# A hybrid encoder trunk: the first half of q's products moved between two pairs of modulation blocks

## The chip, the cores and the metric

The kernel runs on one core of one Trainium2 chip. The metric is the device time of one execution in microseconds (us); lower is better. A core has a matrix engine (TensorE, PE in the profile; its weight loads are PEld), a vector engine (VectorE, DVE), a scalar engine (ScalarE, ACT), a third elementwise engine (GpSimd, POOL) and an engine that issues transfers (SyncE, SP). Each works through its own instructions in the order in which they stand, and waits where an instruction needs a result of another engine or a transfer.

## What is computed

Two layers over 256 tokens of width 1024. In each layer a vector `c` gives six modulation vectors, the normalised input is scaled and shifted with two of them, and projected by one wide matrix; q and k of the recurrent branch are the first columns of that projection.

```python
cond = jax.nn.silu(c)
for l in range(DEPTH):
    mod = cond @ w_ada[l] + b_ada[l]
    shift1, scale1, gate1, shift2, scale2, gate2 = ...
    h = rms_norm(x, norm1_g[l]) * (1 + scale1) + shift1
    proj = h @ w_in[l] + b_in[l]
    ...
    x = x + gate1 * (merged @ w_out[l])
    h2 = rms_norm(x, norm2_g[l]) * (1 + scale2) + shift2
    x = x + gate2 * hierarchical_moe(h2, ...)
return rms_norm(x, final_norm_g)
```

Between the projection and `merged` stand a short convolution and a gated recurrence on q, k and v, a grouped attention, and a merge of both; the mixture of experts has 32 experts of width 512.

## The kernel before

A weight matrix is kept in tiles of 1 MB (128 partitions x 2048 numbers). `plan` is one list of all weight loads in the order of their use; `pump` issues them on SP's queue as buffers come free. A load also waits for the load that stands eight places ahead of it (the four that ACT issues at the start are among the eight).

**The opening of layer 0.** `shift1` and `scale1` are each two blocks of 512 columns; `FIRST = (0, 2, 1, 3)` is the order of the four blocks: the first half of shift, the first half of scale, then the two second halves. For each block `ada_fast` runs `ada_sums` (L415): two weight tiles, four products of 32 x 512 with each, into the tile `pada`; ACT copies it to the buffer `t` (L431). `columns` (L438) turns such a row into four columns of a tile `pcol` with two-column products on PE, and `ada_put` (L449) adds the bias and writes them to `c1b` on DVE. PE also transposes the input (`turn_rows`, L487, four tiles `pxt`) and spreads the norm's factor over the partitions (`spread`, L687).

**build(ks)** makes the modulated input for the row blocks k of 128 channels, as a high part `hh` and a low part `hl` (what the high part's rounding leaves): DVE scales the transposed rows (L700), ACT adds the shift and rounds (L701). For even k, DVE makes the low part (L706); for odd k, ACT makes the full sum (L703) and POOL subtracts the high part from it (in `low`, L501). Blocks 0 to 3 need the modulation blocks 0 and 2, blocks 4 to 7 need 1 and 3. In the order below `hh` and `hl` are the buffers R_141 and R_142 of the kernel before.

**dense(1)** does one step of the projection. `prep` takes half a weight tile through one of two spare buffers (R_143 and R_144): ACT rounds it to its high part (L520), DVE and POOL each subtract one half to get the low part (L501). Then PE makes 24 products (`chan`, L560): high weight x `hh`, high weight x `hl`, low weight x `hh`, each for two column groups o and four blocks k. Two steps (`kh` 0 and 1) cover blocks 0 to 3 and 4 to 7 of one pair of column groups. The first four steps of layer 0 are ordered q's first pair with blocks 0 to 3, q's second pair with blocks 0 to 3, and then both with blocks 4 to 7. Of the two weight tiles the first serves the first two steps. In this text the four are steps 1 to 4. When a pair is complete, `fin_qk` runs: ACT adds a bias (L592), ACT and DVE do a convolution of five taps (L594, L596), and ACT the silu (L598).

What sets the order: PE and SP follow the order in which the code is written (`MANUAL`); ACT, DVE and POOL are ordered by a scheduler, which `tc.high_priority` tells what to put first. `MIX` lists, for each layer, how many dense steps stand between the other pieces of work; its first entry for layer 0 is 3, of which one step was already done in the opening. PSUM tiles come in two groups of four buffers: tag "f" for products and modulation sums, tag "c" for the rest (`pxt` among them).

Of the kernel before, what the change touches and what calls it, by code (L numbers as in the profile page):

```python
# [18 lines left out]
P = 128  # L19
# [47 lines left out]
def trunk(ctx, tc, x, c, b_ada, b_in, mlstm_norm_g, norm2_g, final_g,  # L67
# [211 lines left out]
    for l in range(depth):  # L279
        if l == 0:  # L280
            for b in FIRST:
                plan_ada(0, b)
        else:
            plan_ada(l, EARLY[0])
        for it in stream(l):
            if it[0] in DENSE:
                sh = (8, 256) if it[0] == "akv" else (4, 512)
                add((it[0], l, *it[1:]), in_t[l, W_IN.index(it)].rearrange("p (k c) -> p k c", k=sh[0]), sh)
            elif it[0] == "r":
                plan_ada(l, it[1])  # L290
            else:
                plan_ada(l + 1, it[1])
# [116 lines left out]

    def ada_sums(l, b):  # L410
        pb = ps.tile([P, 512], F32, tag="f", name="pada")
        for h in range(2):
# [14 lines left out]

    def ada_fast(b):

        t = rot("fast", 5, 0, 2, 512)  # L430
        A.copy(t, ada_sums(0, b))  # L431
        return t

    def columns(t):

        pc = ps.tile([P, 512], F32, tag="f", name="pcol")
        for j in range(4):
            T.matmul(pc[:, 2 * j:2 * j + 2], lhsT=t[:, P * j:P * j + P], rhs=ones[:, 0:2], start=True, stop=True)  # L438
        return pc[:, 0:8].rearrange("p (j o) -> p j o", o=2)[:, :, 0]
# [7 lines left out]

    def ada_put(c1, cols, b, t):
        V.tensor_tensor(c1[:, 4 * b:4 * b + 4], columns(t), cols[:, 80 + 4 * b:84 + 4 * b], op=ALU.add)  # L449

# [39 lines left out]
    def mixer(l, p):  # L490
# [185 lines left out]
        if l == 0:  # L676
            fast = {FIRST[0]: ada_fast(FIRST[0])}
        else:
# [30 lines left out]
        if l == 0:  # L709
            cols = p["cols"]  # L710
            spread()
            fast[FIRST[1]] = ada_fast(FIRST[1])
            for b in FIRST[:2]:
                ada_put(c1, cols, b, fast[b])
            build(range(4))
            for b in FIRST[2:]:
                fast[b] = ada_fast(b)
            with tc.high_priority():
                for b in FIRST[2:]:
                    ada_put(c1, cols, b, fast[b])  # L720
                build(range(4, 8))
            dense(1)
            withhold([("a", s) for s in ONCE])
# [320 lines left out]
        for i, w in enumerate(MIX[l].split()):  # L1044
            if w.isdigit():
                for _ in range(int(w) - (i == 0)):
                    step()
# [548 lines left out]
```

## Time and profile before

| | |
|---|---|
| median of 3 runs | 1459.84 us (1457.97 to 1459.91) |
| the profiled execution's own time | 1458.14 us |
| its span, first to last instruction | 1456.4 us |
| mean granted TensorE clock | 0.974 |
| PE busy | 1324.0 us (91%) |
| DMA | 521.29 MB, mean 358 GB/s |

A profile is one execution. Its rows name the engine, the line, the operation, output and inputs by the program's names, and how many instructions stand in the row. In a timeline a row begins with its start and its length, and ends with the idle time of its engine just before and what released it. In views by stretch the columns are the busy time of each engine with its count of records, the granted clock (1.00 is 2.4 GHz, 0.50 is 1.2 GHz), the busy share of the DMA engines and what they moved. A product in 32-bit mode shows as two records; the rounded ones of L560 show as one.

### The profile page before, as it was taken

To read this page: it belongs to the slowest core of one execution; us is meant where nothing else is said; L and a number is where in the kernel's file an instruction comes from. 1 tells how busy PE (TensorE), PEld (TensorE's weight loads), DVE (VectorE), ACT (ScalarE), POOL (GpSimd) and SP (SyncE) were. 2 spreads that over 40 slices of the span, in tenths; PEclk is the share of its full clock that TensorE was granted. 3 is DMA by queue.
4 is the path that set the end of the run, shared out by engine and by line. 5 is a ranking of instruction groups with operands and counts; after the bars stand their busy time and mean duration, and the time that the engine had idled before them with its cause. 6 is when DMAs were issued, how large, how long until landed. Compare 5 with 4: busy or idle time off the path is not lost. (4 is left out here: it accounts for less than half of the span.)

```text
span 1456.4 us, 19790 instructions
## 1 busy us (share of the span) xinstructions
PE 1324.0 (91%) x7836; PEld 771.7 (53%) x7837; DVE 615.3 (42%) x1376; ACT 403.4 (28%) x755; POOL 264.5 (18%) x297
## 2 busy tenths in 40 slices
PE   6899999799999989789889999997999998987996
PEld 3788779734443434234359788893443443433432
DVE  3686756613323223212268776653323232223223
ACT  3636564411111101101046366542111111101111
POOL 2553336200000000000045533550000000000000
PEclk9999999899999999999999999998999999999998
DMA  9866594899999999999996556459999999999995
GB/s 385 350 267 251 234 366 170 329 387 424 426 427 424 425 428 425 425 384 416 424 415 239 227 188 241 178 232 370 426 425 424 428 425 425 427 425 424 373 427 231
DMA packets 50148, 521.29 MB, mean 358 GB/s; under 512 B 6656, under 2 KB 6656, under 8 KB 9344
## 3 DMA queue, kind: packets, MB, share of 16 engines
q1 hardware_dynamic: 48576, 515.94, 85.9%
q0 software_dynamic: 608, 2.14, 0.4%
q10 hardware_dynamic: 864, 1.85, 0.3%
q8 instruction: 65, 1.06, 0.3%
q14 instruction: 35, 0.29, 0.1%
HBM read 518.86 MB, written 1.05 MB: 357 GB/s over the span
## 5 line engine op out<-in xcount | busy, mean ns | idle before, releaser
L1300 PE MATMUL pgu<-arena 128*64 128x512 f32 x1376 | 325.9, 599 | 19.7 <-DMA arena<-in_gate_t_dram 12.6
L1300 PEld LDWEIGHTS pgu<-arena 128*64 128x64 f32 x1376 | 104.4, 138 | 232.1 <-issue 196.5
L1324 PE MATMUL pd<-arena 128*64 128x512 f32 x800 | 195.5, 595 | 21.8 <-ACT arena L1315 21.8
L1309 DVE SCALAR_TENSOR_TENSOR arena<-pgu,wsl,arena 128x512 f32<-128x512 f32 x32 | 24.0, 751 | 381.1 <-PE pgu L1300 381.1
L1256 POOL TENSOR_TENSOR arena<-oh,arena 128x256 f32<-128x256 f32 x32 | 19.5, 615 | 728.4 <-DVE oh L1250 465.5
L579 PE MATMUL pd<-R,R 128*128 128x256 f32 x1056 | 138.6, 290 | 3.3 <-DVE arena L619 1.7
L579 PEld LDWEIGHTS pd<-R,R 128*128 128x128 f32 x1056 | 132.3, 196 | 10.9 <-issue 6.1
L560 PE MATMUL pd<-R,R 128*128 128x256 f32 x1008 | 132.0, 289 | 4.7 <-ACT R L520 3.6
L501 POOL TENSOR_TENSOR R<-arena,R 128x512 fp32r<-128x512 f32 (+1 forms) x74 | 113.6, 1536 | 121.9 <-ACT R L520 88.7
L1324 PEld LDWEIGHTS pd<-arena 128*64 128x64 f32 x800 | 60.0, 137 | 137.5 <-issue 107.9
L560 PEld LDWEIGHTS pd<-R,R 128*128 128x128 f32 x1008 | 125.2, 194 | 13.9 <-issue 5.3
L1335 DVE TENSOR_TENSOR y<-pd,arena 128x512 f32<-128x512 f32 x64 | 44.1, 692 | 198.0 <-PE pd L1324 167.1
L1336 ACT CAST yh<-y 128x512 fp32r<-128x512 f32 x64 | 39.6, 619 | 235.5 <-DVE y L1335 235.5
L1300 PE MATMUL pgu<-B,arena 128*64 128x512 f32 x352 | 97.5, 594 | 2.3 <-DMA B<-in_up_t_dram 1.7
L501 DVE TENSOR_TENSOR R<-arena,R 128x512 fp32r<-128x512 f32 (+1 forms) x82 | 72.8, 896 | 61.1 <-ACT R L520 52.8
L1272 PE MATMUL pG<-oh,X 128*128 128x256 f32 x512 | 73.3, 306 | 16.1 <-DVE oh L1250 15.9
L1347 DVE TENSOR_TENSOR xs<-xs,psc 128x512 f32<-128x512 f32 x128 | 79.4, 681 | 17.6 <-PE psc L1344 17.6
L1272 PEld LDWEIGHTS pG<-oh,X 128*128 128x128 f32 x512 | 69.5, 211 | 27.4 <-issue 26.5
L520 ACT CAST R<-arena 128x1024 fp32r<-128x1024 f32 x66 | 68.8, 1042 | 50.1 <-PE pd L579 23.2
L1315 ACT COPY arena<-pat 128x512 f32<-128x512 f32 x32 | 18.7, 586 | 210.2 <-PE pat L1314 210.2
L1300 PE MATMUL pgu<-X,arena 128*64 128x512 f32 x320 | 72.3, 593 | 4.5 <-DMA X<-in_up_t_dram 4.5
L1308 ACT ACTIVATE arena<-pgu 128x512 f32<-128x512 f32 x32 | 19.1, 597 | 192.5 <-PE pgu L1300 192.5
(319 smaller groups left out, 1652.8 us busy)
## 6 DMA issues: line engine op xcount, KB each, us to landing
arena<-in_down_t_dram SPq DMA_DIRECT2D x45, 2048.0 KB, 29.4
arena<-in_up_t_dram SPq DMA_DIRECT2D x42, 2048.0 KB, 28.0
arena<-in_gate_t_dram SPq DMA_DIRECT2D x39, 2048.0 KB, 27.2
arena<-in_ada_t_dram SPq DMA_DIRECT2D x31, 1024.0 KB, 6.6
B<-in_up_t_dram SPq DMA_DIRECT2D x12, 2048.0 KB, 31.1
arena<-in_in_t_dram SPq DMA_DIRECT2D x23, 1024.0 KB, 6.5
X<-in_gate_t_dram SPq DMA_DIRECT2D x10, 2048.0 KB, 32.3
X<-in_up_t_dram SPq DMA_DIRECT2D x10, 2048.0 KB, 34.5
```

The costliest lines, as they stand in the source:

```text
L501: eng.tensor_tensor(dst, full, hi.bitcast(F32), op=ALU.subtract)
L520: A.copy(wh, w)
L560: T.matmul(acc[key][o][:, 0:S], lhsT=w[:, kk, P * o:P * o + P], rhs=x_[:, 4 * kh + kk], start=kh == 0 and i == 0 and kk == 0, stop=kh == 1 ...
L579: T.matmul(acc[key][t][:, 0:256], lhsT=x_[:, 4 * kh + kk, P * t:P * t + P], rhs=w[:, kk], start=kh == 0 and i == 0 and kk == 0, stop=kh == ...
L1256: G.tensor_tensor(ow, oh[:, :, 2 * (i % 2):2 * (i % 2) + 2].bitcast(F32), cb[:, :, 2 * i:2 * i + 2].unsqueeze(3).to_broadcast([P, NT, 2, C ...
L1272: T.matmul(pG[:, kk, 0:n], lhsT=x_[:, t, P * k:P * k + P], rhs=oh[:, t, :], start=i == 0, stop=i == 3)
L1300: T.matmul(pg[CAP * e:CAP * e + CAP, :], lhsT=xg[4 * h + kk][:, P * (i % 2) + CAP * e:P * (i % 2) + CAP * e + CAP], rhs=w[e][:, kk, :], st ...
L1309: V.scalar_tensor_tensor(ac.rearrange("p k q -> p (k q)"), pu, wsl[:, 0:1], sl, op0=ALU.mult, op1=ALU.mult)
L1324: T.matmul(pd[n][CAP * e:CAP * e + CAP, :], lhsT=aT[:, 2 * h + kk, CAP * e:CAP * e + CAP], rhs=w[e][:, kk, 512 * n:512 * n + 512], start=h ...
L1335: V.tensor_tensor(y[:, cs], pd, gt2b[:, cs], op=ALU.mult)
L1336: A.copy(yh[:, cs], y[:, cs])
L1347: V.tensor_tensor(xx, xx, pq, op=ALU.add)
```

## The change

The weight tile of q's first half is loaded in fifth place, between the tiles of the first two and of the last two modulation blocks, instead of ninth. The first dense step (step 1) stands between `build(range(4))` and the sums of blocks 1 and 3, and the second (step 2) between their columns and `build(range(4, 8))`. The sums and columns of blocks 1 and 3 use PSUM buffers of tag "c" instead of "f", since steps 1 and 2 hold all four of "f". The mixer's loop does one dense step less in layer 0; layer 1 is as before.

```diff
         if l == 0:
-            for b in FIRST:
+            for b in FIRST[:2]:
+                plan_ada(0, b)
+            add(("q", 0, 0, 0), in_t[0, W_IN.index(("q", 0, 0))].rearrange("p (k c) -> p k c", k=4), (4, 512))
+            for b in FIRST[2:]:
                 plan_ada(0, b)
...
-            if it[0] in DENSE:
+            if l == 0 and it == ("q", 0, 0):
+                pass
+            elif it[0] in DENSE:
...
-    def ada_sums(l, b):
-        pb = ps.tile([P, 512], F32, tag="f", name="pada")
+    def ada_sums(l, b, tag="f"):
+        pb = ps.tile([P, 512], F32, tag=tag, name="pada")
...
-                ada_put(c1, cols, b, fast[b])
+                ada_put(c1, cols, b, fast[b], "f")
             build(range(4))
+            dense(1)
             for b in FIRST[2:]:
-                fast[b] = ada_fast(b)
+                fast[b] = ada_fast(b, "c")
             with tc.high_priority():
                 for b in FIRST[2:]:
-                    ada_put(c1, cols, b, fast[b])
+                    ada_put(c1, cols, b, fast[b], "c")
+            dense(1)
+            with tc.high_priority():
                 build(range(4, 8))
-            dense(1)
...
-                for _ in range(int(w) - (i == 0)):
+                for _ in range(int(w) - (i == 0) * (2 - l)):
```

Lines of the changed kernel are 5 to 7 higher (L415 is L420, L501 is L506, L520 is L525, L560 is L565, L701 is L706), and its R buffers one higher: `hh` is R_142, `hl` R_143, the spare buffers R_144 and R_145.

On PE, before, from the columns of the first two blocks to step 4 (`pada` with B and arena are the sums of blocks 1 and 3, each row of `pd` a third of a step):

```order
L438 MATMUL pcol<-onesr,arena 128x2 x8
L415 MATMUL pada<-B_88,condp 32x512 x8
L415 MATMUL pada<-B_89,condp 32x512 x4
L415 MATMUL pada<-arena,condp 32x512 x4
L438 MATMUL pcol<-onesr,arena 128x2 x8
L560 MATMUL pd<-R_141,R_143 128x256 x8
L560 MATMUL pd<-R_142,R_143 128x256 x8
L560 MATMUL pd<-R_141,R_143 128x256 x8
L560 MATMUL pd<-R_141,R_144 128x256 x8
```

The same stretch of PE in the changed kernel:

```order
L443 MATMUL pcol<-onesr,arena 128x2 x8
L565 MATMUL pd<-R_142,R_144 128x256 x8
L565 MATMUL pd<-R_143,R_144 128x256 x8
L565 MATMUL pd<-R_142,R_144 128x256 x8
L420 MATMUL pada<-B_88,condp 32x512 x4
L420 MATMUL pada<-B_89,condp 32x512 x4
L420 MATMUL pada<-arena,condp 32x512 x8
L443 MATMUL pcol<-onesr,arena 128x2 x8
L565 MATMUL pd<-R_142,R_145 128x256 x8
```

The 24 products of step 1 now stand ahead of all sums of blocks 1 and 3.

On ACT, before, `build(range(4))`, the copies of the sums of blocks 1 and 3, and the begin of `build(range(4, 8))` with the first rounding of weights:

```order
L701 ACTIVATE R_141<-arena,c1b 128x256 x3
L703 ACTIVATE arena<-arena,c1b 128x256
L701 ACTIVATE R_141<-arena,c1b 128x256
L703 ACTIVATE arena<-arena,c1b 128x256
L431 COPY arena<-pada 128x512 x2
L701 ACTIVATE R_141<-arena,c1b 128x256
L520 CAST R_143<-spare 128x1024
```

The same stretch of ACT in the changed kernel:

```order
L706 ACTIVATE R_142<-arena,c1b 128x256
L525 CAST R_144<-B_88 128x1024
L525 CAST R_145<-B_88 128x1024
L706 ACTIVATE R_142<-arena,c1b 128x256 x2
L708 ACTIVATE arena<-arena,c1b 128x256
L706 ACTIVATE R_142<-arena,c1b 128x256
L708 ACTIVATE arena<-arena,c1b 128x256
L436 COPY arena<-pada 128x512 x2
L706 ACTIVATE R_142<-arena,c1b 128x256
L525 CAST R_144<-spare 128x1024
```

Both roundings of q's first tile (for steps 1 and 2) moved into `build(range(4))`, behind its first block.

On POOL, before, from the last table of the setup: the low parts of blocks 1 and 3 (128x256), small fills, and the low weights of step 1:

```order
L380 IOTA desc 128x8
L501 TENSOR_TENSOR R_142<-arena,R_141 128x256 x2
L1043 MEMSET arena 128x8
L590 MEMSET arena 128x2
L591 MEMSET arena 128x2
L590 MEMSET arena 128x2
L591 MEMSET arena 128x2
L501 TENSOR_TENSOR R_143<-spare,R_143 128x512
```

And in the changed kernel:

```order
L385 IOTA desc 128x8
L506 TENSOR_TENSOR R_144<-B_88,R_144 128x512
L506 TENSOR_TENSOR R_145<-B_88,R_145 128x512
L506 TENSOR_TENSOR R_143<-arena,R_142 128x256 x2
L1050 MEMSET arena 128x8
```

The two subtractions for the low weights of steps 1 and 2 moved ahead of the low parts of blocks 1 and 3.

## Rows read from the trace of the kernel before

**Rows 1.** The page's busy times over the whole span: engine, busy us, share of the span, instructions.

```profile
PE 1324.0 (91%) x7836; PEld 771.7 (53%) x7837; DVE 615.3 (42%) x1376; ACT 403.4 (28%) x755; POOL 264.5 (18%) x297
```

**Rows 2.** The timeline of SP's queue in the opening: each row is the issue of one to four weight tiles.

```profile
0.85 2.05 SPq L206 DMA_DIRECT2D arena<-in_ada_t_dram  x4
6.15 4.13 SPq L206 DMA_DIRECT2D B<-in_ada_t_dram  x3
13.75 0.33 SPq L206 DMA_DIRECT2D arena<-in_ada_t_dram  x1
14.12 0.43 SPq L206 DMA_DIRECT2D spare<-in_in_t_dram  x1
```

**Rows 3.** The view of transfers, of the stretches that hold the issue of the fifth (6.15 us), the eighth (13.75 us) and the ninth weight tile (14.12 us, q's first): count, size, and us from issue to landing.

```profile
B<-in_ada_t_dram SPq DMA_DIRECT2D x1, 1024.0 KB, 13.0
...
arena<-in_ada_t_dram SPq DMA_DIRECT2D x1, 1024.0 KB, 12.9
...
spare<-in_in_t_dram SPq DMA_DIRECT2D x1, 1024.0 KB, 16.4
```

**Rows 4.** The timeline of PE from the columns of the first two blocks to the next pair of steps (a row of 72 is three steps), and the sums of one block further on.

```profile
20.64 1.95 PE L438 MATMUL pcol<-onesr,arena 128*128 128x2 f32 x16
22.52 2.87 PE L415 MATMUL pada<-B,condp 128*32 128x512 f32 x24
26.71 1.07 PE L415 MATMUL pada<-arena,condp 128*32 128x512 f32 x8 [1.32 <-DMA arena<-in_ada_t_dram]
27.70 1.95 PE L438 MATMUL pcol<-onesr,arena 128*128 128x2 f32 x16
32.10 10.90 PE L560 MATMUL pd<-R,R 128*128 128x256 f32 x72 [2.45 <-ACT R L520]
42.93 1.93 PE L748 MATMUL pg<-R,pk 128*32 128x256 f32 x32
...
48.14 8.87 PE L560 MATMUL pd<-R,R 128*128 128x256 f32 x72
...
76.76 1.92 PE L415 MATMUL pada<-arena,condp 128*32 128x512 f32 x16
```

**Rows 5.** The timeline of ACT in both builds.

```profile
23.60 1.31 ACT L701 ACTIVATE R<-arena,c1b 128x256 fp32r<-128x256 f32 x3 [2.23 <-DVE arena L700]
...
25.21 0.49 ACT L701 ACTIVATE R<-arena,c1b 128x256 fp32r<-128x256 f32 x1
...
31.02 1.03 ACT L520 CAST R<-spare 128x1024 fp32r<-128x1024 f32 x1
...
33.16 0.49 ACT L701 ACTIVATE R<-arena,c1b 128x256 fp32r<-128x256 f32 x1
```

**Rows 6.** The timeline of POOL in both builds.

```profile
25.38 0.72 POOL L501 TENSOR_TENSOR R<-arena,R 128x256 fp32r<-128x256 f32 x1 [20.71 <-ACT arena L703]
26.32 0.73 POOL L501 TENSOR_TENSOR R<-arena,R 128x256 fp32r<-128x256 f32 x1 [0.21 <-ACT arena L703]
...
32.12 1.78 POOL L501 TENSOR_TENSOR R<-spare,R 128x512 fp32r<-128x512 f32 x1 [2.98 <-ACT R L520]
33.87 0.91 POOL L501 TENSOR_TENSOR R<-arena,R 128x256 fp32r<-128x256 f32 x1
34.75 1.72 POOL L501 TENSOR_TENSOR R<-spare,R 128x512 fp32r<-128x512 f32 x1
36.44 0.73 POOL L501 TENSOR_TENSOR R<-arena,R 128x256 fp32r<-128x256 f32 x1
```

**Rows 7.** The timeline of DVE: the first rows of `build(range(4, 8))`, and the convolution of q's first pair and of k's first pair.

```profile
30.08 1.27 DVE L700 SCALAR_TENSOR_TENSOR arena<-pxt,A,arena 128x256 f32<-128x256 f32 x3
...
44.50 4.21 DVE L596 SCALAR_TENSOR_TENSOR arena<-arena,pk 128x256 f32<-128x256 f32 x8 [0.60 <-ACT arena L594]
...
59.80 3.14 DVE L596 SCALAR_TENSOR_TENSOR arena<-arena,pk 128x256 f32<-128x256 f32 x4
...
62.94 2.11 DVE L596 SCALAR_TENSOR_TENSOR arena<-arena,pk 128x256 f32<-128x256 f32 x4
```

**Rows 8.** The view by stretch: stretch, its length, busy time of PE, PEld, DVE, ACT and POOL with counts, granted clock, DMA share, GB/s.

```profile
26.70:29.65 2.95, 2.94 (x24) 2.02 (x24) 0.16 (x1) 0.60 (x2) 0.79 (x6) 1.00 1.03 419
29.65:32.10 2.45, 0.00 (x1) 0.00 (x1) 2.34 (x8) 1.50 (x3) 0.00 (x0) 0.54 1.00 415
32.10:36.30 4.20, 4.20 (x19) 4.20 (x20) 2.69 (x4) 3.23 (x7) 4.17 (x3) 0.50 1.02 389
36.30:42.93 6.63, 6.63 (x55) 6.50 (x53) 1.39 (x2) 2.56 (x3) 4.22 (x4) 0.97 1.03 408
63.52:66.86 3.34, 0.00 (x0) 0.00 (x1) 2.38 (x5) 2.58 (x5) 1.73 (x4) 1.00 0.10 39
66.86:260.00 193.14, 186.92 (x1481) 158.40 (x1481) 134.04 (x330) 101.29 (x194) 85.55 (x73) 0.99 0.67 259
300.00:775.00 475.00, 436.67 (x2208) 193.54 (x2205) 145.96 (x267) 77.77 (x140) 29.19 (x49) 0.99 1.00 419
```

**Rows 9.** The waits of PE from 42 to 100 us, then those of ACT from 42 to 70 us: who waited for whom, us in total, times, the longest.

```profile
PE pada L415 <- ACT arena L592: 3.3, 1, 3.3
...
ACT arena L598 <- DVE arena L596: 4.0, 3, 2.2
ACT R L520 <- PE pd L560: 1.8, 1, 1.8
```

More of the change, by code (lines that the diff above doesn't have):

```diff
@@ L426, in ada_part, with ada_fast, columns @@
         return ph, pw
-    def ada_fast(b):
+    def ada_fast(b, tag):
         t = rot("fast", 5, 0, 2, 512)
-        A.copy(t, ada_sums(0, b))
+        A.copy(t, ada_sums(0, b, tag))
         return t
-    def columns(t):
-        pc = ps.tile([P, 512], F32, tag="f", name="pcol")
+    def columns(t, tag="f"):
+        pc = ps.tile([P, 512], F32, tag=tag, name="pcol")
         for j in range(4):
@@ L446, in shift_put, with ada_put @@
         V.tensor_tensor(sh2c[:, s], columns(sums_at), b3[:, s], op=ALU.add)
-    def ada_put(c1, cols, b, t):
-        V.tensor_tensor(c1[:, 4 * b:4 * b + 4], columns(t), cols[:, 80 + 4 * b:84 + 4 * b], op=ALU.add)
+    def ada_put(c1, cols, b, t, tag):
+        V.tensor_tensor(c1[:, 4 * b:4 * b + 4], columns(t, tag), cols[:, 80 + 4 * b:84 + 4 * b], op=ALU.add)
     def ada_sum(parts):
@@ L676, in mixer @@
         if l == 0:
-            fast = {FIRST[0]: ada_fast(FIRST[0])}
+            fast = {FIRST[0]: ada_fast(FIRST[0], "f")}
         else:
@@ L711, in mixer @@
             spread()
-            fast[FIRST[1]] = ada_fast(FIRST[1])
+            fast[FIRST[1]] = ada_fast(FIRST[1], "f")
             for b in FIRST[:2]:
-                ada_put(c1, cols, b, fast[b])
+                ada_put(c1, cols, b, fast[b], "f")
             build(range(4))
+            dense(1)
             for b in FIRST[2:]:
-                fast[b] = ada_fast(b)
+                fast[b] = ada_fast(b, "c")
             with tc.high_priority():
                 for b in FIRST[2:]:
-                    ada_put(c1, cols, b, fast[b])
+                    ada_put(c1, cols, b, fast[b], "c")
+            dense(1)
+            with tc.high_priority():
                 build(range(4, 8))
-            dense(1)
             withhold([("a", s) for s in ONCE])
```

## The prediction

> **What bounds the kernel now.** I read the page's busy times first: PE is busy for 91% of the span [rows 1], so one looks for the places where it is not, and the change touches only the opening. There I read, in this order: SP's queue and the landings, PE's timeline, and then what ACT and POOL do in the two builds.
>
> The fifth weight tile is issued at 6.15 us and lands 13.0 later, at 19.2; the eighth lands at 13.75 + 12.9 = 26.65, and the ninth, q's first, at 14.12 + 16.4 = 30.5 [rows 2, 3]. PE stops for the eighth tile until 26.71, ends the sums of the fourth modulation block at 27.78, makes the columns until 29.65, and has nothing to do until step 1 begins at 32.10 [rows 4]. Steps 1 to 3 are one row of 72 products from 32.10 to 42.93, where 72 products further on take 8.87. The difference is the clock: from 29.65 to 32.10 it averages 0.54, and 19 products take 4.20 us at 0.50, which is 0.221 each; at full clock one costs 8.87/72 = 0.123 [rows 4, 8].
>
> Two chains matter for what follows. `build(range(4))` ends on POOL: the low part of block 3 is ready at 26.32 + 0.73 = 27.05 [rows 6]. `build(range(4, 8))` begins on DVE at 30.08, 2.30 after the last sum, and ends on POOL with the low part of block 7 at 36.44 + 0.73 = 37.17, 7.09 after its begin [rows 4, 6, 7]. That chain is hidden today: step 3, the first that reads blocks 4 to 7, stands behind the 48 products of steps 1 and 2.
>
> From 42.93 on, the end of step 3, ACT and DVE set the pace: the convolution of q's first pair follows at once, ACT waits for DVE three times, and PE waits 3.3 us for the bias step of k's last pair, at 66.86 [rows 7, 9]. No transfer ends a wait there. So what moves the end of step 3 moves, I hold, the rest: after 66.86 PE is busy for 186.92 of 193.14 us, and the experts' stretch runs with its DMA share at 1.00 on buffers that the mixer releases [rows 8], so both shift as a whole.
>
> **The change, part by part.**
>
> *The loads.* q's tile takes the fifth place and lands at about 19.2, before anyone wants it. Each tile of the last two modulation blocks moves down one place; the last one lands at 30.5 instead of 26.65, 3.85 later. Even with nothing else in the way, the last sum would end at 30.5 + 1.0 = 31.5, the second build begin at 33.8 and its low parts be ready at 40.9, and step 3 finish with its last 13 products at 42.5. It ends at 42.93 now. So the most that the new place can give is 0.4 us: the second build, hidden before, is the path after the change.
>
> *ACT.* Both roundings of q's first tile now stand behind block 0 of the first build. They cost 1.03 each [rows 5]: they run from 24.1 to 26.15, and the high part of block 3, written at 25.21 + 0.49 = 25.70 now, comes at 27.8.
>
> *POOL.* The two subtractions for the low weights, 1.78 and 1.72, stand ahead of the low parts of blocks 1 and 3 [rows 6]. They start when the first rounding is done, 25.1, and end at 28.6; the two low parts follow with 0.72 and 0.73, so block 3 is ready at 30.1 instead of 27.05.
>
> *PE, step 1.* It starts at 25.1, but its fourth product needs block 3's high part (27.8) and its twelfth block 3's low part (30.1). 13 of the 24 products (the twelfth, four more with low parts of the input, eight with low weights) are still to come at 30.1: 1.6 us at full clock, 2.9 at half. From 20.64 to 27.8 PE has only two-column products and some single ones. In the kernel before the clock fell at about 29.8, behind 1.3 us without work and a stretch of sums and two-column products; I take it that it falls here too, and comes back once step 1 and the sums run without a gap. Step 1 then ends at 33.0, and at 31.7 with the clock up.
>
> *PE, the sums.* They stand behind step 1 in PE's order, so what was done while tiles arrived is done afterwards: two blocks at 1.92 each [rows 4] are 3.8 us at full clock, from 33.0 to 36.8. Their last tile has been there since 30.5; the wait for it is gone, and what is late next is PE itself. Before, the sums ended at 27.78: 9.0 us earlier.
>
> *The second build.* With the same distances it begins at 36.8 + 2.30 = 39.1 and ends at 46.2. In between PE does step 2 (24 products, 3.0 us, hidden) from 38.8 to 41.8 and the first 11 products of step 3 by about 42.8 (block 7's high part, 33.16 + 0.49 = 33.65 before, is 3.57 behind the build's begin [rows 5, 7]). Then it waits for POOL. From 46.2 on 13 products remain, 1.6 at full clock and 2.9 at half after a wait of more than 3 us. I take 2.2 between the two: step 3 ends at 48.4, against 42.93. That is 5.5 us later.
>
> *Behind it.* In ACT's new order both bias steps of k's first pair stand ahead of a table load that lay between them. The eight convolution steps of that pair took from 59.80 to 65.05, 5.25 us, where those of q's first pair took 4.21 [rows 7]. That can give up to 1.0; I take 0.7.
>
> The sum is 5.5 - 0.7 = 4.8 us. On the profiled execution's 1458.14 that gives 1462.9; the median of the runs shown is 1459.84, 1.7 higher, and on it the forecast is 1464.6.
>
> *What moved without a price.* The tiles of tag "c" for sums and columns take buffers that the first build has released before step 1 ends, so they add no wait; if one did, it would fall into the same stretch. The loads behind the ninth keep their places in SP's queue, and the layer-0 loop does one step less because that step has been done. Some later tiles sit in other buffers; I bound that by 1 us to either side, the half of the spread of the three runs.
>
> **A rule and the rows.** The clock fell at about 29.8 in the row 29.65 to 32.10 (0.54), though PE is recorded busy for 2.94 of the 2.95 us ahead of it [rows 8]. The Trainium skill, "TensorE: Matmul & The Clock Gate", Part 1, says that the half-rate state is the default and returns after idleness, and that the moment depends on how the monitor's phase lies to the program, so that it differs from run to run. Read as idleness alone, step 1's short waits would leave the clock up; the row shows a fall behind little idleness, so I go by the row and keep the other as a rival.
>
> **The rivals.**
>
> *The clock stays up.* For it: no wait inside step 1 is longer than 2.4 us. Against it: the fall at 29.8 behind 1.3 us. Step 1 ends at 31.7, the sums at 35.5, the second build at 44.9, step 3 at 46.5: 3.6 later, less 0.7, or 1462.7.
>
> *The clock stays down through the sums.* For it: it needed from 32.10 to past 36.3 to come back [rows 8]. The sums take 7.7 instead of 3.8 and step 3's end costs 2.9: the build ends at 50.1, step 3 at 53.0, 10.1 later, less 0.7: 1469.2. Against it: by 33 PE has worked without a gap for 3 us.
>
> *The pause swallows it.* PE stands still from 63.52 to 66.86, 3.34 us [rows 8]. If part of the chain that ends it does not hang on q's first pair, the delay fills that pause: 4.8 - 3.3 = 1.5, or 1461.3. Against it: ACT's and DVE's waits from 42.93 on are for one another and for PE [rows 9].
>
> *The other side: the products fill the wait.* If POOL's and ACT's new order costs nothing that the wait for the last tile does not cover, the sums end with the landing at 31.5, and step 3 at 42.5: 0.4 sooner, 1459.4, and with PE busy where it idled the clock may stay up and give 1.9 us more (19 products at 0.10). It decides when block 3's low part is ready by 27.5 or so, since then step 1 and block 1's sums end before 30.5. The order on POOL speaks against it: 3.5 us of subtractions stand ahead.
>
> **How the numbers follow.** A change of 0.2%, 2.9 us, is about what a measurement of this kernel can tell from none. Forecast 0.54 (1464.6, its own range 1462.8 to 1467.0); clock up 0.14, half of it above 1462.8; clock down 0.10; pause 0.11; other side 0.11, of which 0.05 is faster by more than 0.2%. Slower: 0.54 + 0.07 + 0.10 = 0.71, say 0.70; faster 0.05; within 0.2% 0.25. The range takes in the pause below and most of what lies between the forecast and the slow clock above: 1460.5 to 1468.0, which leaves out the other side and the most of the slow clock, 2 in 10.
>
> **What would show it.** In the profile of the changed kernel: q's tile landing near 19 us and the last modulation tile near 30.5; two rounding rows of 1.03 on ACT near 24 to 26; POOL's 128x512 rows ahead of its 128x256 rows, the second of these ending near 30; step 1's last product near 33; the sums of blocks 1 and 3 without a wait for a transfer, ending near 36.8; DVE's second build beginning near 39; a wait of PE for POOL of some 3 us inside step 3; and the gates (the row at 42.93 before) starting near 48. I am wrong if the second build begins before 35, or if the row that stood at 66.86 has moved by less than 2 us.

## The result, and the profile after

The changed kernel takes 1467.33 us (median of 5 runs, 1466.04 to 1468.71) where the kernel before took 1459.00 beside it (1457.35 to 1459.91): a ratio of 1.0057, 95% interval 1.0044 to 1.0071, or 8.3 us slower. A second measurement gave 1468.09 against 1458.25, ratio 1.0061 (1.0046 to 1.0076). The forecast was 1464.6 with a range of 1460.5 to 1468.0: right in sign and in range, 2.7 us short in size. Against the kernel before beside it the change cost 8.3 us where 4.8 were forecast, since that kernel's median was 0.8 below the 1459.84 on which the forecast stands. The profiled execution took 1468.14, span 1466.5, which is 10.1 more than that of before.

SP's queue after, answering to [rows 2], and the landing of its fifth and its ninth tile, answering to [rows 3], from the view of transfers:

```profile
6.03 0.33 SPq L206 DMA_DIRECT2D B<-in_in_t_dram  x1
6.41 3.75 SPq L206 DMA_DIRECT2D B<-in_ada_t_dram  x2
13.61 0.80 SPq L206 DMA_DIRECT2D arena<-in_ada_t_dram  x2
```

```profile
B<-in_in_t_dram SPq DMA_DIRECT2D x1, 1024.0 KB, 13.0
...
arena<-in_ada_t_dram SPq DMA_DIRECT2D x1, 1024.0 KB, 15.1
```

q's tile lands at 6.03 + 13.0 = 19.0, the last modulation tile at 13.98 + 15.1 = 29.1. The timeline of PE over the stretch of [rows 4]:

```profile
23.61 0.58 PE L565 MATMUL pd<-R,R 128*128 128x256 f32 x1 [2.50 <-ACT R L525]
24.96 0.98 PE L565 MATMUL pd<-R,R 128*128 128x256 f32 x2 [0.78 <-ACT R L706]
26.16 1.65 PE L565 MATMUL pd<-R,R 128*128 128x256 f32 x6 [0.21 <-ACT R L706]
28.02 3.83 PE L565 MATMUL pd<-R,R 128*128 128x256 f32 x15 [0.21 <-POOL R L506]
31.77 2.16 PE L420 MATMUL pada<-B,condp 128*32 128x512 f32 x16
33.76 1.89 PE L420 MATMUL pada<-arena,condp 128*32 128x512 f32 x16
35.58 1.05 PE L443 MATMUL pcol<-onesr,arena 128*128 128x2 f32 x8
36.97 1.02 PE L443 MATMUL pcol<-onesr,arena 128*128 128x2 f32 x8 [0.34 <-DVE c1b L454]
37.86 5.92 PE L565 MATMUL pd<-R,R 128*128 128x256 f32 x35
45.54 2.83 PE L565 MATMUL pd<-R,R 128*128 128x256 f32 x13 [1.76 <-POOL R L506]
48.30 2.43 PE L755 MATMUL pg<-R,pk 128*32 128x256 f32 x32
```

Step 1 is the first four rows; each begins with a wait for ACT or POOL. The sums follow without a wait for a transfer, the second build lies under the row at 37.86, and POOL ends the wait in step 3, as the prediction had it. The gates start at 48.30 (42.93 before, 48.4 forecast). The rows of ACT, POOL and DVE that answer to [rows 5 to 7] (three timelines, in this order):

```profile
22.53 1.98 ACT L525 CAST R<-B 128x1024 fp32r<-128x1024 f32 x2
```

```profile
23.64 3.46 POOL L506 TENSOR_TENSOR R<-B,R 128x512 fp32r<-128x512 f32 x2 [18.97 <-ACT R L525]
27.05 1.60 POOL L506 TENSOR_TENSOR R<-arena,R 128x256 fp32r<-128x256 f32 x2
...
44.77 0.71 POOL L506 TENSOR_TENSOR R<-arena,R 128x256 fp32r<-128x256 f32 x1
```

```profile
38.43 1.27 DVE L705 SCALAR_TENSOR_TENSOR arena<-pxt,A,arena 128x256 f32<-128x256 f32 x3
```

Both roundings and both subtractions stand ahead of blocks 1 and 3. The stretches, with the columns of [rows 8]: step 1, the sums, and step 3's last 13 products.

```profile
23.61:31.85 8.24, 7.04 (x28) 5.63 (x32) 3.51 (x3) 3.01 (x6) 5.01 (x4) 0.50 1.00 417
31.85:35.60 3.75, 3.75 (x33) 0.86 (x33) 0.00 (x0) 0.59 (x1) 0.11 (x1) 0.94 1.00 405
...
45.54:48.37 2.83, 2.83 (x17) 2.61 (x21) 0.33 (x1) 1.42 (x2) 0.00 (x0) 0.57 1.01 420
```

The clock (column behind the five engines) is down through step 1, back for the sums, and down again for most of step 3's last 13 products.

The prediction's frame ends here: it held that what moves the end of step 3 moves the rest. Laying the two traces over each other, instruction by instruction on PE (my own subtraction of start times, 7836 in each), the shift is 5.4 us at the gates, 6.5 behind the pause at 66.86, 7.5 at 178, 9.7 from 262 on, and 9.6 at the end (times of the kernel before). Two places behind the pause are new. PE's timeline of the changed kernel around 174, and at the first step behind the mixer:

```profile
173.78 1.07 PE L420 MATMUL pada<-spare,condp 128*32 128x512 f32 x8
175.73 1.06 PE L420 MATMUL pada<-arena,condp 128*32 128x512 f32 x8 [0.89 <-DMA arena<-in_ada_t_dram]
...
263.75 0.44 PE L1095 MATMUL pxa<-ident,arena 128*128 128x128 f32 x2 [2.13 <-POOL arena L1086]
...
264.79 4.46 PE L584 MATMUL pd<-R,R 128*128 128x256 f32 x24
```

In the kernel before, the same sums are one row of 1.92 without a wait, and the same place behind the mixer reads:

```profile
167.25 1.92 PE L415 MATMUL pada<-arena,condp 128*32 128x512 f32 x16
...
255.52 0.44 PE L1088 MATMUL pxa<-ident,arena 128*128 128x128 f32 x2 [1.47 <-POOL arena L1079]
...
256.41 3.12 PE L579 MATMUL pd<-R,R 128*128 128x256 f32 x24
```

So PE waits 0.9 for a weight tile, then 0.7 longer for POOL, and 24 products behind that wait take 1.3 longer. The opening does not touch these places; something that it set in motion does.

### The profile page after: what moved, and what is told of

Same layout as the page of the kernel before. It is cut to its first block, busy times and chain, and to the rows that moved or that the text cites. A ratio compares the mean times of both kernels' runs of the same rounds, so it can differ in the third digit from the quotient of the medians.

```text
span 1466.5 us, 19781 instructions
## 1 busy us (share of the span) xinstructions
PE 1324.0 (90%) x7836; PEld 770.5 (53%) x7837; DVE 615.7 (42%) x1376; ACT 404.0 (28%) x755; POOL 265.3 (18%) x297
## 5 line engine op out<-in xcount | busy, mean ns | idle before, releaser
L1307 PE MATMUL pgu<-arena 128*64 128x512 f32 x1296 | 306.3, 597 | 19.3 <-DMA arena<-in_gate_t_dram 12.6
L1331 PE MATMUL pd<-arena 128*64 128x512 f32 x880 | 212.6, 595 | 21.8 <-ACT arena L1322 21.8
L1307 PEld LDWEIGHTS pgu<-arena 128*64 128x64 f32 x1296 | 98.1, 137 | 217.8 <-issue 190.8
L565 PE MATMUL pd<-R,R 128*128 128x256 f32 x1008 | 136.8, 294 | 8.2 <-ACT R L525 4.1
L1331 PEld LDWEIGHTS pd<-arena 128*64 128x64 f32 x880 | 65.8, 137 | 148.8 <-issue 119.3
L584 PE MATMUL pd<-R,R 128*128 128x256 f32 x1056 | 137.4, 288 | 3.3 <-DVE arena L624 1.7
L565 PEld LDWEIGHTS pd<-R,R 128*128 128x128 f32 x1008 | 128.2, 197 | 18.7 <-issue 5.7
L506 POOL TENSOR_TENSOR R<-arena,R 128x512 fp32r<-128x512 f32 (+1 forms) x72 | 109.9, 1529 | 132.7 <-ACT R L525 107.1
L1307 PE MATMUL pgu<-B,arena 128*64 128x512 f32 x432 | 115.5, 593 | 5.0 <-DMA B<-in_up_t_dram 3.9
L506 DVE TENSOR_TENSOR R<-arena,R 128x512 fp32r<-128x512 f32 (+1 forms) x80 | 69.4, 876 | 58.8 <-ACT R L525 48.0
L1279 PEld LDWEIGHTS pG<-oh,X 128*128 128x128 f32 x512 | 69.2, 210 | 27.3 <-issue 26.5
L525 ACT CAST R<-arena 128x1024 fp32r<-128x1024 f32 x64 | 66.7, 1043 | 53.7 <-PE pd L584 31.5
L1283 ACT ACTIVATE arena<-pG,sh2c 128x256 f32<-128x256 f32 x64 | 30.4, 475 | 151.3 <-DVE arena L1285 151.3
## 6 DMA issues: line engine op xcount, KB each, us to landing
arena<-in_down_t_dram SPq DMA_DIRECT2D x50, 2048.0 KB, 29.6
```

Source lines behind the costliest of these rows:

```text
L506: eng.tensor_tensor(dst, full, hi.bitcast(F32), op=ALU.subtract)
L525: A.copy(wh, w)
L565: T.matmul(acc[key][o][:, 0:S], lhsT=w[:, kk, P * o:P * o + P], rhs=x_[:, 4 * kh + kk], start=kh == 0 and i == 0 and kk == 0, stop=kh == 1 ...
L584: T.matmul(acc[key][t][:, 0:256], lhsT=x_[:, 4 * kh + kk, P * t:P * t + P], rhs=w[:, kk], start=kh == 0 and i == 0 and kk == 0, stop=kh == ...
L1279: T.matmul(pG[:, kk, 0:n], lhsT=x_[:, t, P * k:P * k + P], rhs=oh[:, t, :], start=i == 0, stop=i == 3)
L1283: A.activation(xg[k][:, 0:n], pG[:, kk, 0:n], AF.Identity, bias=sh2c[:, k:k + 1])
```

## The experiments

Each median is of 5 to 12 runs. A ratio is to the kernel before on the same chip; kernels with the same time of the kernel before ran on the same chip.

| kernel | median us | before us | ratio, 95% interval | gates start | 24 products behind the mixer |
|---|---|---|---|---|---|
| changed | 1467.33 | 1459.00 | 1.0057 (1.0044 to 1.0071) | 48.30 | 4.46 |
| e1 loads alone | 1463.61 | 1457.85 | 1.0040 (1.0026 to 1.0053) | 45.14 | 4.28 |
| e2 low part first | 1466.11 | 1457.85 | 1.0054 (1.0041 to 1.0068) | 45.33 | 5.34 |
| e3 block 1 first | 1465.88 | 1457.85 | 1.0057 (1.0043 to 1.0071) | 45.43 | 4.39 |
| e5 order alone | 1467.61 | 1457.85 | 1.0070 (1.0056 to 1.0084) | 49.81 | 4.62 |
| changed, again | 1468.09 | 1458.25 | 1.0061 (1.0046 to 1.0076) | 50.71 | 4.62 |
| e8 changed, old buffers | 1463.31 | 1458.25 | 1.0034 (1.0022 to 1.0046) | 46.76 | 3.12 |
| e10 before, new buffers | 1461.56 | 1458.25 | 1.0029 (1.0018 to 1.0040) | 42.76 | 4.45 |
| e11 e2, e3 and e8 together | 1460.63 | 1458.25 | 1.0014 (1.0005 to 1.0022) | 43.17 | 3.13 |
| e12 before, parameters early | 1453.68 | 1457.80 | 0.9974 (0.9964 to 0.9984) | 42.62 | 3.11 |
| e13 changed, parameters early | 1463.06 | 1457.80 | 1.0032 (1.0021 to 1.0043) | 47.16 | 3.11 |
| e6 changed, filled wait | 1466.49 | 1457.80 | 1.0060 (1.0046 to 1.0075) | 45.78 | 4.42 |
| e7 before, filled waits | 1461.51 | 1457.80 | 1.0029 (1.0015 to 1.0043) | 47.87 | 3.13 |

### Parts of the change by themselves

**e1, the loads alone.** The order of loads of the changed kernel in the code of the kernel before.

```diff
-            for b in FIRST:
+            for b in FIRST[:2]:
+                plan_ada(0, b)
+            add(("q", 0, 0, 0), ...)
+            for b in FIRST[2:]:
                 plan_ada(0, b)
```

> The kernel before with the new order of loads alone: q's first tile is fifth, all products stand where they stood before. Theory (the order of the work costs the time, the loads do not): the last modulation tile lands near 30.5, the sums end near 31.5, the second build begins near 33.8, and step 3 ends between 42.5 and 44.5, against 42.93 before and 48.3 in the changed kernel; the time is 0 to 2 us above before. Rival (the late modulation tiles cost it): step 3 ends at 46 or later, and the time is 5 to 8 us above before.

The time agrees with the rival, the trace with neither. PE's wait for the last tile ends at 29.14 instead of 26.71, and the gates start 2.2 later: the late tile costs 2.2 where PE stands waiting for it. By 262 us the shift is 6.1 us, and the two new places of the changed kernel are there, though no product was moved. My theory had no account of that.

**e5, the order alone.** The order of work of the changed kernel, with q's tile loaded ninth.

```diff
-            for b in FIRST[:2]:
-                plan_ada(0, b)
-            add(("q", 0, 0, 0), ...)
-            for b in FIRST[2:]:
+            for b in FIRST:
                 plan_ada(0, b)
+            add(("q", 0, 0, 0), ...)
```

> The changed order of the work with the old order of loads: q's first tile is ninth again and lands near 30.5, behind both last modulation tiles. Theory (what stands behind step 1 waits for its end): step 1 cannot begin before q's weights are rounded, near 31.5, and ends at 34.5 to 36; the sums end at 38.5 to 40, step 3 at 50 to 52, and the time is 9 to 13 us above before, 2 to 4 above the changed kernel. Rival (the late modulation tiles cost the time, the order of the products does not): the time is within 2 us of before.

Step 1 runs from 30.00 to 35.10, step 3 ends at 49.8, and the time is 9.8 above before: the theory's case, at its lower end. It is not clearly above the changed kernel (the intervals overlap), and its trace shows two reasons. The scheduler gave ACT the order of the kernel before in the stretch behind the gates, so the shift stays at 6.9 from the gates through the pause at 66.86 [rows 8], where the changed kernel's grows by 1.2. And behind the pause it falls from 6.9 to 5.2, because PE's work there ran at a granted clock of 1.00, in the kernel before at 0.62 (in the changed kernel at 0.65). The same work in the kernel before, then in e5:

```profile
66.86:71.30 4.44, 4.44 (x24) 1.84 (x25) 4.00 (x9) 1.71 (x4) 1.60 (x1) 0.62 0.89 264
```

```profile
73.73:76.60 2.87, 2.87 (x24) 1.43 (x25) 2.46 (x5) 1.88 (x4) 1.60 (x1) 1.00 0.60 194
```

**e2, block 3's low part ahead of the second weight chunk**, by holding the rounding and subtractions of that chunk behind it.

```diff
-            with tc.high_priority(offset=PREP):
+            with ExitStack() as after:
+                if held_by and len(spare) == 0:
+                    after.enter_context(tc.issue_after(held_by[0].ins))
+                else:
+                    after.enter_context(tc.high_priority(offset=PREP))
```

> The changed kernel, with the rounding of q's second two weight chunks and their subtraction on GpSimd held behind the low part of block 3, so that step 1 finds its input sooner. Theory (POOL's and ACT's order inside the first build is part of the cost): block 3's low part is ready near 26.5 to 27 instead of 28.6, step 1 ends 1 to 2.5 us sooner than in the changed kernel, and so does step 3; the time is 1 to 2.5 us below the changed kernel, that is 6 to 7 us above before. Rival (the low weights, not block 3, end step 1, or the clock sets it): step 1 ends where it did, and the time is within 0.7 us of the changed kernel.

**e3, block 1's sums ahead of step 1.**

```diff
+            fast[FIRST[2]] = ada_fast(FIRST[2], "c")
             dense(1)
-            for b in FIRST[2:]:
-                fast[b] = ada_fast(b, "c")
+            fast[FIRST[3]] = ada_fast(FIRST[3], "c")
```

> The changed kernel, with the sums of block 1 ahead of step 1 instead of behind it, where their tiles have landed and PE waits for step 1's input; only block 3's sums follow step 1. Theory (two blocks of sums that used to run while tiles arrived are now done behind step 1, and the second build hangs on them): the last sum comes about 1.9 to 2.5 us sooner than in the changed kernel (31.8 + 3.8 there), the second build and step 3 with it, and the time is 2 to 4 us below the changed kernel. Rival (the second build is set by step 1's own end or by its engines' queues): step 3 ends within 0.7 us of the changed kernel's.

In both traces the mechanism is as expected: e2 ends step 1 at 30.1 instead of 31.85, e3 ends the sums at 33.8 instead of 35.65, and the gates start 3.0 and 2.9 sooner. Of that 1.0 is the clock in step 3's last 13 products, which took 2.83 in the changed kernel's profile and 1.81 and 1.82 here. e8 (below), which has the changed kernel's order, has 1.82 there too and its gates at 46.76; against it e2 and e3 gain 1.4 and 1.3. In the times nothing is clear of the noise: the medians are 8.3 and 8.0 us above the kernel before on the same chip, the changed kernel's two 8.3 and 9.8, so the gains that were expected in time (1 to 2.5 us and 2 to 4) are not shown. In e2 one sees a part of why: its shift behind the pause is 2.7 less than the changed kernel's, but behind the mixer it waits 3.19 for POOL instead of 2.13, and its 24 products take 5.34.

### Where the rest comes from

So the next question was what e1, e2, e3 and e5 have in common with the changed kernel. It is the buffers. Seven buffers take the loads in turn, four slices of the arena and three that the profile calls B, and an eighth, spare; `pump` gives each load the first one that is free in the order of the program. A piece of `MIX` ("hold") withdraws the three B buffers in the mixer: each is lost when the tile in it is done. Following `pump` through the program, q's first tile in B instead of spare turns the row of buffers by one, and the second half of `gm`'s first tile (a later projection) comes to lie in B instead of spare: the third B buffer is lost five tiles earlier, and the loads behind it have one buffer less for a while. In e5 q's first tile lies in spare as before, but step 1 is done with it sooner, and by that the row turns a few loads later; the second half of `gm`'s first tile lies in B there too. SP's queue, first of the kernel before, then of the changed kernel, from the same load on (its shift is 6.5 here):

```profile
139.59 0.33 SPq L206 DMA_DIRECT2D arena<-in_ada_t_dram  x1
140.43 0.33 SPq L206 DMA_DIRECT2D spare<-in_ada_t_dram  x1
150.81 0.33 SPq L206 DMA_DIRECT2D arena<-in_in_t_dram  x1
151.67 0.33 SPq L206 DMA_DIRECT2D arena<-in_ada_t_dram  x1
```

```profile
146.13 0.33 SPq L206 DMA_DIRECT2D spare<-in_ada_t_dram  x1
157.35 0.33 SPq L206 DMA_DIRECT2D arena<-in_ada_t_dram  x1
158.20 0.33 SPq L206 DMA_DIRECT2D arena<-in_in_t_dram  x1
167.12 0.33 SPq L206 DMA_DIRECT2D spare<-in_ada_t_dram  x1
```

The second load comes 16.9 later instead of 6.5, the fourth 15.5: each waits for one release more. The tile that PE waits for at 174.84 is the next load, issued at 167.97 and landed 7.7 later.

**The changed kernel again**, beside the next three.

> The changed kernel once more, beside the next three on one chip. Two runs of the same program: the time is again 7 to 10 us above before. In its trace the shift against before is again 5 to 7 us at k's last pair (73 us) and 8 to 10 behind 270 us, if the growth between them is the kernel's; if it was one execution's clock, the shift stays near 6.5.

The growth behind the pause repeats: 9.4 there, 12.4 from 262 on, which is 3.1 more (3.2 in the first profile). Both shifts are above what was expected (5 to 7, and 8 to 10), because the opening differs: the clock was 0.50 already in the sums of the second block (3.64 instead of 1.92), so step 1 began at 25.96 and the gates at 50.71, although the median is the same within 0.8.

**e8, the changed kernel with the old buffers.**

```diff
         if kind == "z":
+            if key in (("q", 0, 0, 1), ("k", 0, 0, 0), ("k", 0, 0, 1), ("akv", 0, 0), ("aq", 0, 0, 0),
+                       ("aq", 0, 0, 1), ("ada", 1, 0, 0)):
+                return False
```

> The changed kernel, with the buffer called spare kept from the seven loads behind it in the plan, so that every load from the tenth on lands in the buffer that it has in the kernel before. Theory (the load order costs a second time, through the buffers: the second half of gm's first tile now sits in a buffer that is withdrawn when it is done, so that each load behind waits for one release more): the loads issued at 157.35 and 167.12 in the changed kernel come some 10 us sooner, PE's wait for a transfer at 174.8 is gone, the wait of DVE for the packed parameters near 257 falls from 4.0 to 3 or less, and the time is 2 to 3.5 us below the changed kernel. Rival (only the clock's phase made the growth behind 73 us): the time is within 0.8 us of the changed kernel.

**e10, the kernel before with the new buffers**, and nothing else.

```diff
         kind, s = slot
+        if key == ("q", 0, 0, 0):
+            return slot == ("a", 9)
         if kind == "z":
```

> The kernel before, with one thing changed: q's first tile lands in a buffer of the modulation instead of spare, by which every load from the tenth on lands in the buffer that it has in the changed kernel. Nothing in the order of the work differs. Theory (the buffers cost it): the opening to 73 us is as before within 0.5 us, then PE waits about 0.9 for a transfer near 167 and the shift grows to 2 to 3.5 us by 270, and the time is 2 to 3.5 us above before. Rival (the clock's phase): the time is within 0.8 us of before.

Both come out for the buffers. e8 is 4.8 us below the changed kernel beside it (2 to 3.5 expected) and 5.1 above before; its shift is 5.1 behind the pause, 5.2 at 262, so the growth of 3.1 to 3.2 is gone. The 4.8 is more than the buffers: e8's opening also ran at a higher clock than both profiles of the changed kernel (gates at 46.76, not 48.30 or 50.71), with the same order of work and waits within 0.02 us of the first profile's. e10 leaves the opening as it was (gates at 42.76) and costs 3.3 us; the interval is 2.6 to 5.8. Its PE rows carry both marks of the changed kernel:

```profile
167.17 1.07 PE L417 MATMUL pada<-spare,condp 128*32 128x512 f32 x8
169.16 1.06 PE L417 MATMUL pada<-arena,condp 128*32 128x512 f32 x8 [0.93 <-DMA arena<-in_ada_t_dram]
...
257.01 0.44 PE L1090 MATMUL pxa<-ident,arena 128*128 128x128 f32 x2 [1.96 <-POOL arena L1081]
...
258.05 4.45 PE L581 MATMUL pd<-R,R 128*128 128x256 f32 x24
```

**e11, all three costs taken out**: the edits of e2, e3 and e8.

> Loads in the new order, block 1's sums ahead of step 1, the low part of block 3 ahead of the second weight chunk, and the buffers of the kernel before from the tenth load on: the change with each of its three costs taken out. Theory (order on POOL and ACT, sums behind step 1, and the buffers are what it costs): step 1 ends at 29.5 to 30.5, the sums with the last tile at 31.5 to 32.5, step 3 at 42.5 to 44.5, and the time lies between 0.5 us below and 2.5 us above before. Rival (the late modulation tiles cost it whatever the order is): the time is 4 us or more above before.

The expected 0 to 2.5: step 1 ends at 29.6, the sums at 31.5, the gates start at 43.17, and the time is 2.4 us above before. e8 and e11 differ by the order of the work (the edits of e2 and e3; nine loads only change places among the B buffers by it): 2.7 us in time, 3.6 at the gates. Of the 2.4 that are left the trace shows 1.3: the shift is 0.2 at the gates and 1.8 at 73 us (ACT's order, below), 0.5 at 178, since a wait of PE of 0.46 for DVE, at 172.93 in the kernel before, and short gaps behind it are gone, and 1.3 at the end. So the change with its three costs removed still does not gain.

### The wait behind the mixer

Behind the mixer DVE waits for layer 1's packed parameters, a transfer that POOL issues when the router's logits of layer 0 are done. The rows of DVE in the kernel before and in the changed kernel:

```profile
252.14 0.60 DVE L726 TENSOR_TENSOR c1b<-c,pk 128x16 f32<-128x16 f32 x1 [2.93 <-DMA pk<-in_packs_dram]
```

```profile
260.80 0.17 DVE L733 TENSOR_TENSOR c1b<-c,pk 128x16 f32<-128x16 f32 x1 [4.01 <-DMA pk<-in_packs_dram]
```

The transfer takes 3.8 us before and 4.9 after. With the old buffers two expert tiles (up) are issued at 243.67 and 254.28, and the first lands at 251.48; with the new ones they are issued at 246.62 and 251.24, and the second lands at 260.30. In all twelve profiles but those of e12 and e13 the parameters land 0.3 to 0.7 us behind the up tile that was issued last before them; so where that tile stands sets the wait.

**e12 and e13** take that wait out: 36 columns that the logits need are copied aside, and the scheduler then issues the load some 26 us earlier.

```diff
         G.memset(vx[:, :, :, P:P + 1], 1.0)
+        br = small("br", 36)
+        G.tensor_copy(br, p["br"])
...
-        V.tensor_tensor(lc, pL[0][:, 72:108], p["br"], op=ALU.add)
+        V.tensor_tensor(lc, pL[0][:, 72:108], br, op=ALU.add)
```

> The kernel before, with the router's bias (36 columns of the packed parameters) copied aside at the start of each layer, so that layer 1's packed parameters can be loaded before the logits are done. Theory (DVE's wait of 2.93 for that load is what PE's wait of 1.47 at 255 us hangs on): DVE no longer waits for the parameters, PE's wait falls to 0.7 or less, and the time is 0.7 to 1.5 us below before. Rival (the chain from the product itself sets that wait): PE still waits more than 1.2, and the time is within 0.5 us of before.

> The changed kernel with the same copy. Theory (behind the changed buffers two up tiles share the transfer engines with the packed parameters; the longer wait, and the slow clock of the 24 products behind it, are the second part of the growth behind 73 us): DVE's wait of 4.0 is gone, PE's wait of 2.1 falls to 0.9 or less, the 24 products behind it take 3.1 instead of 4.5, and the time is 2 to 3.5 us below the changed kernel; its distance to the kernel before with the same copy is 6 to 8 us. Rival (that stretch is slow for another reason): the 24 products still take over 4 us, and the time is 0 to 1.5 below the changed kernel.

PE's timeline of e12, then of e13:

```profile
254.53 0.44 PE L1090 MATMUL pxa<-ident,arena 128*128 128x128 f32 x2 [0.52 <-POOL arena L1081]
...
255.40 3.11 PE L579 MATMUL pd<-R,R 128*128 128x256 f32 x24
```

```profile
261.83 0.44 PE L1097 MATMUL pxa<-ident,arena 128*128 128x128 f32 x2 [0.52 <-POOL arena L1088]
...
262.71 3.11 PE L584 MATMUL pd<-R,R 128*128 128x256 f32 x24
```

The wait falls to 0.52 in both, and the products are at full clock. **e12 is the version that beats both kernels**: 1453.68 us, 4.1 below before (2.3 to 5.2), where 0.7 to 1.5 was expected. Only 1.0 of that is at the place itself (the shift of PE's instructions against before at 262 us); the rest comes in steps between 530 and 1370 us, and its cause is open. e13 is 5.0 below the changed kernel's second median, which is of another chip (2 to 3.5 expected); the place itself accounts for 3.0 (2.13 + 4.46 against 0.52 + 3.11). The distance between e13 and e12 is 9.4 us, more than the 6 to 8 expected.

### The clock

**e6 and e7** fill waits with products of 128 columns whose result nobody reads.

```diff
+        def fill(n):
+            pf = ps.tile([P, 512], F32, tag="f", name="pfill")
+            for _ in range(n):
+                T.matmul(pf[:, 0:P], lhsT=onesr, rhs=onesr, start=True, stop=True)
...
+            fill(30)
             build(range(4))
```

> The changed kernel, with 30 products of 128 columns, whose result nobody reads, between the columns of the first two blocks and step 1, where PE waits 2.5 us. Theory (the slow clock is a part of step 1's cost): the clock stays at 1.00 through step 1, its last 15 products take 1.9 instead of 3.83, it ends 1.5 to 2.2 us sooner, and the time is 1 to 2.5 us below the changed kernel. Rival (the clock falls whatever PE does there): step 1 ends where it did or up to 1 us later, and the time is from 0.5 below to 1 us above the changed kernel.

> The kernel before, with such unread products in its two waits: 12 between the sums of blocks 1 and 3 and 30 between the columns and step 1. Theory (the 10.90 us of steps 1 to 3 are 2.0 too long by the clock alone): the 72 products take 8.9 to 9.6, step 3 ends 1.3 to 2 us sooner, and the time is 1 to 2 us below before. Rival (the clock falls all the same): the 72 products take 10.5 or more, and the time is from 0.5 us below to 1 us above before.

The theory fell in both, and neither rival has all its numbers. The view by stretch of e6 from its second block's sums to step 1's end, then three stretches of e7 from the columns on:

```profile
16.60:20.00 3.40, 3.38 (x28) 1.82 (x28) 0.52 (x2) 0.59 (x1) 0.00 (x0) 1.00 1.02 424
...
22.00:26.50 4.50, 4.50 (x24) 4.50 (x23) 4.25 (x7) 4.39 (x8) 2.90 (x2) 0.50 1.02 419
```

```profile
28.10:30.00 1.90, 1.87 (x16) 1.04 (x16) 0.00 (x0) 0.58 (x1) 0.21 (x2) 1.00 1.01 418
30.00:31.00 1.00, 1.00 (x8) 1.00 (x8) 0.16 (x1) 0.00 (x0) 0.23 (x3) 0.67 1.01 418
...
32.00:38.00 6.00, 6.00 (x30) 6.00 (x29) 4.70 (x9) 4.40 (x8) 3.90 (x3) 0.50 1.04 391
```

In e6 the clock falls from 1.00 to 0.50 at 22 us in the middle of the unread products, with PE recorded busy for 5.38 of the 5.40 us since 16.6 (spreading, sums, 16 records of two-column products from 19.12 to 21.07, then the unread ones). The 30 products then last until 26.5, and step 1, now without waits, ends at 30.5, 1.3 sooner than in the changed kernel; the time is not to be told from the changed kernel's. The profile shows one reason: the shift is 2.8 at 73 us, where the changed kernel has 6.5, but from 117.0 to 121.5 us e6's products ran at a clock of 0.57 behind a wait of 1.74 for DVE, where the changed kernel's ran at 1.00 behind the same wait of 1.74, and the shift is 7.4 behind them. In e7 the clock falls between 30 and 31 us, the 30 unread products take 6.64 where the wait was 2.45, step 1 begins at 37.92 instead of 32.10 (1.4 of it because the last tile came later), the 72 products take 10.02, and the time is 3.7 above before.

## Why the prediction was right, and where it was short

*The loads.* q's tile at 19.0 as forecast; the last modulation tile at 29.1, not 30.5. In the changed kernel that is without effect, since PE asks for it only at 33.76. The argument that the second build becomes the path held: after the sums, every step of it can be seen.

*ACT and POOL.* The order and the lengths are as forecast (1.98 for both roundings, 3.46 for both subtractions, 1.60 for the low parts behind them), 1.5 sooner throughout because PE's transposes and the sums of the second block ran at a higher clock (1.86 and 1.92 us, in the kernel before 3.46 and 2.69); in the second profile they did not, and step 1 begins 0.9 later than forecast. e2 shows what the order on POOL is worth at the gates: 3.0 against this profile, with the clock, and 1.4 against e8's.

*Step 1 and the sums.* Step 1 ended at 31.85 (33.0 forecast), at the slow clock, as the row of [rows 8] had suggested; the sums took 3.8 as forecast and at a clock of 0.94, so "clock down through the sums" is out. e3 shows the price of having one block of them behind step 1: 1.9 at the last sum, and at the gates 2.9 against this profile, 1.3 against e8's.

*The second build and step 3.* From the last sum to DVE's begin 2.8 instead of 2.30: the columns of block 3 waited 0.34 for DVE to read those of block 1, and the row before them is 8 products of its own. The build took 7.05 to its last low part (7.09 forecast). Step 3's last 13 products took 2.83, mostly at the slow clock (2.2 taken). Its end came 5.4 later than before (5.5 forecast). This part of the sum was right to 0.1, with errors of up to 1.2 in its parts that cancelled. That it is so close is luck: three more profiles with this order (the changed kernel again, e8 and e13) have the gates at 50.71, 46.76 and 47.16, which is 3.8 to 7.8 later than before, and they differ by the clock.

*Behind it.* The term had the wrong sign: -0.7 forecast, +1.2 measured (from 5.4 at the gates to 6.5 behind the pause; 0.4 of it is the gates themselves, 2.43 us at a slower clock instead of 1.93). ACT's new order does put both bias steps of k's first pair ahead of the table load, but it also puts a rounding ahead of ACT's part of the convolution in each half of q's second pair. The convolution of that pair took 3.48 + 2.50 with a subtraction between, from 55.78 to 62.29, 6.5 us; in the kernel before it ran from 50.73 to 56.06, 5.3. DVE after:

```profile
55.78 3.48 DVE L601 SCALAR_TENSOR_TENSOR arena<-arena,pk 128x256 f32<-128x256 f32 x3
...
59.79 2.50 DVE L601 SCALAR_TENSOR_TENSOR arena<-arena,pk 128x256 f32<-128x256 f32 x5
```

k's first pair, from which the gain was to come, took 5.6 instead of 5.25. e11, whose gates are at 43.17, has the same two lengths there (3.48 and 2.49), and its shift grows from 0.2 at the gates to 1.8 at 73 us; e5, whose ACT kept the order of the kernel before there, is 6.9 late at the gates and still 6.9 at the pause. So this is ACT's order and not the delay.

*The step that failed.* "Some later tiles sit in other buffers; I bound that by 1 us to either side, the half of the spread of the three runs." It measured 3.3 us by e10, and 3.1 to 3.2 as the growth of the shift between 73 and 262 us in e10 and in both profiles of the changed kernel; e8's 4.8 holds a faster opening besides. The bound was taken from the spread of a measurement, which says nothing of a mechanism, while the mechanism could have been read: `pump` decides on buffers in the order of the program, before anything runs. With it falls the sentence that behind 66.86 both shift as a whole. e8, without the turned buffers, is 5.1 us above before, where the other terms were forecast at 4.8: 2.7 for the order of the work (e8 against e11) and 2.4 that e11 leaves. With the 3.3 of e10 that makes 8.4, where the changed kernel measured 8.3 and 9.8.

*The range.* That the result lies in it is luck in part. Its upper end was drawn for a slow clock through the sums, which did not come; what filled it are the buffers, bounded at 1 us, and the wrong sign of the term behind the gates.

*The rivals.* The other side (the products fill the wait) is what e11 comes nearest to, with the order on POOL changed and block 1 first; it is still 2.4 above before. The pause swallowed nothing, neither in the changed kernel nor in e5, whose delay is longer: PE's wait there is 3.67 and 3.36 us, and 3.35 before. In e6 alone it is shorter, 2.17.

## What to carry to other kernels

A load that is moved in a list can turn the allocation of buffers behind it, and where buffers are withdrawn later, one tile in the wrong buffer can delay the loads of a whole stretch: follow the allocator through the program before and after, and hold the load times against the waits 100 us on. Work that is moved into a wait is paid by what stood behind it in the queue; ask first what chain becomes the path then, here a build of 7 us that had been hidden. And a term that one bounds by the noise of a measurement has not been looked at.

## What the runs showed of the hardware that was not expected

The clock behind a wait: over the fourteen profiles of this study, the 24 products behind the mixer ran at full clock (3.11 to 3.13 us, granted clock 1.00) in six of the seven with a wait of 1.47 or less ahead of them (the seventh is e5: 1.47, then 4.62), and slower (4.28 to 5.34, granted clock 0.53 to 0.69) in all seven with a wait of 1.96 to 3.19. A wait that is up to 1.7 longer was so followed by up to 2.2 more. What set e5 apart is open. Nor does the wait alone decide: behind the same wait of 1.74 for DVE the clock fell in e6, at 117 us, and stayed at 1.00 in the changed kernel.

The clock without a wait: in e6 it fell after PE had been recorded busy for 5.38 of 5.40 us. The Trainium skill, "TensorE: Matmul & The Clock Gate", Part 1, lets the half rate return after idleness; by that the unread products would have held the clock, and these rows say that they did not. What part the two-column products just ahead of them have in the fall, no run here shows.
